# A two-layer mLSTM and retention trunk: head 0 reordered, its gate chain in pieces, and a first stage in another order

## The chip, the cores and the metric

The kernel runs on one core of one Trainium2 chip. The core has a matmul engine (PE, with its weight loads shown apart as PEld), a vector engine (DVE), an activation engine (ACT), a general engine (POOL) and a queue engine (SP) that here issues every transfer. The metric is the device time of one execution in microseconds. Each engine has its own stream of instructions and runs it in order; a semaphore holds an instruction back until its inputs are there.

## The reference

Two layers; each conditions a normalisation on a vector c, projects to gates, queries, keys and values, runs eight heads and projects back with a residual. Four heads are mLSTM, four are retention.

```python
for l in range(DEPTH):
    ada = silu(c) @ w_ada[l] + b_ada[l]
    shift, scale, gate = jnp.split(ada, 3, axis=-1)
    h = rmsnorm(x, norm_g[l]) * (1 + scale) + shift
    mq, mk, mv, mo, mz, mi, mf, rq, rk, rv, rz = split_cols(h @ w_in[l])
    qk = silu(causal_dwconv(concat([mq, mk]), conv_w[l], conv_b[l]))
    cell = mlstm_chunkwise(q, k, mv, mi + b_igate[l], mf + b_fgate[l])
    y_m = sigmoid(mo) * head_layernorm(cell, gn_m[l]) * silu(mz)
    ret = retention_chunkwise(rotary(rq), rotary(rk), rv)
    y_r = head_layernorm(ret, gn_r[l]) * silu(rz)
    x = x + gate * (concat([y_m, y_r]) @ w_out[l])
return rmsnorm(x, final_g)
```

Sequence 1024, model width 1024, head width 256, all float32. The mLSTM gates need, per head, running sums of log-sigmoids and a running maximum over the sequence; the kernel works in chunks of 256 tokens.

## The kernel before

Every product of float32 matrices is three matmuls of split operands (`mm3`, L134 to L136): each operand is cast to a high part (`split_to`, L574, mostly on ACT) and a low part, the rest of the subtraction (L575, mostly on POOL). A weight panel is a raw tile of 128 rows by 512 columns with its `wH` and `wL`. The hidden state `hT` lies transposed, eight slices of 128 model columns (k) by two halves of 512 tokens.

*The first stage* (L992 to L1067, layer 0) makes `hT` while the adaptive shift and scale come in. `ada_load` brings w_ada in four groups of 256 columns, `ada_group` (L216 to L226) accumulates each with multiply-adds by the activated c on DVE, `ada_sums` (L231) adds over partitions with matmuls, and `finish_gsh` (L201 to L204) turns the sums into `gsh`, shift and scale by column. The rows of x are squared with an accumulator on ACT (`squares`, L984), their root is taken over DVE and POOL (`row_rstd`, L923 to L926), the rows are scaled (`norm_scale`, L282 on ACT, L284 on DVE) and transposed by PE (L289), and each slice is split (`norm_split`: L295 or L297 with shift and scale, the high part L299 on ACT, the low part L300 on POOL). A step `first(half, k)` then multiplies one slice of one half by the z and o weights of head 0's first 128 columns, six matmuls of 512 columns. x comes in two halves, `xts[0]` and `xts[1]`. All of this stage's instructions are written out in order for all engines; behind it only PE's order is written out, and the other engines' orders come from the scheduler by the readiness that it computes.

*Units and launches.* Behind the first stage PE's stream is made of units: a projection of 128 columns (`proj_units`) is four units of 12 matmuls of 512 columns. `run_units` runs them one by one; each unit is a tick of a clock. `launch(generator, delay)` lets another generator take one step at each tick, from `delay` ticks on, up to its next `yield`; a `yield n` pauses it for n ticks. So the side work of a head (the gate chain, the value splits, the attention) is laid between the projections of the same or the next head.

*Head 0 of a layer*, in PE's order: z and o of the first 128 columns; z of the second 128 (`wz1`, L1077); the value units together with the gate columns (`v0_units` with `load_v0`, L1079); the gate chain launched (L1080); o of the second 128 (L1081); the query path and the key path with their convolutions (`conv_silu`: ACT L587, four DVE multiply-adds L592 and L594, ACT L596, DVE L597; keys split at L574, L575 and stored to DRAM); the value splits (`v0_splits`, L560 to L564, scaled by the gates) launched between the query and the key path with a delay of 2 (L1097); the attention launched with a delay of 2 (L1105); and head 1's paths go on beside it.

`gate_chain` (L417) runs on four partitions by 512: activations with Ln and Exp on ACT (L426 to L434), then for two halves some fifteen DVE operations each (L441 to L460, two sums and a maximum as scans among them), `yield 12`, and then transposes by PE (L468) and the small tables made from them. `attention` (L695) has, for four chunks j, `scores(j)` (matmuls of keys by queries, DVE products with the decay `dm`, L727 to L730, and a split into `sH` and `sL`), `values(j)` (matmuls of `sH`, `sL` by the values, and from the second chunk by the state) and `update(j)` (the state). In the attention it says

```python
scores(0)
yield 1
scores(1)
yield 1
for j in range(NCH):
    values(j)
```

Of the kernel before, what the change touches and what calls it, by code (L numbers as in the profile page):

```python
# [11 lines left out]
F32 = mybir.dt.float32  # L12
# [57 lines left out]
def tile_hybrid_trunk(ctx, tc, x, c, positions, w_ada, b_ada, norm_g, w_in, conv_w, conv_b,  # L70
# [92 lines left out]
    def load_cols_raw(l):  # L163
        rows = wt("rows", P, 2)
        Q.dma_start(rows[0:8, :], norm_g[l].rearrange("(r c) -> r c", c=P))
        Q.dma_start(rows[8:24, :], conv_b[l].rearrange("(r c) -> r c", c=P))
        Q.dma_start(rows[24:88, :], conv_w[l].rearrange("t (r c) -> (t r) c", c=P))
        Q.dma_start(rows[88:96, :], gn_m[l].rearrange("(r c) -> r c", c=P))
        Q.dma_start(rows[96:104, :], gn_r[l].rearrange("(r c) -> r c", c=P))
        Q.dma_start(rows[104:128, :], b_ada[l].rearrange("(r c) -> r c", c=P))  # L170
# [5 lines left out]
    def load_cols(l, rb):  # L176
        rows, bg = rb
        pt = ps_a()
        PE.transpose(pt[:, 0:P], rows, ident)
        cl = cst.tile([P, P], F32, tag=f"cols{l}", name=f"cols{l}")  # L180
        V.tensor_copy(cl, pt[:, 0:P])
        V.tensor_scalar(cl[:, 88:96], cl[:, 88:96], 0.25, None, ALU.mult)
        V.tensor_scalar(cl[:, 96:104], cl[:, 96:104], 0.5, None, ALU.mult)
        cols[l] = (cl, bg)
# [31 lines left out]
    def ada_group(raws, acc, parts):  # L216
        for part in parts:
            for a in range(2):
                kk = part * 2 + a
                for which in range(2):  # L220
                    aw = acc[:, which * 256:(which + 1) * 256]
                    rr = raws[part * 2 + which][:, a, :]
                    if kk == 0:
                        V.tensor_scalar(aw, rr, cact[:, 0:1], None, ALU.mult)
                    else:
                        V.scalar_tensor_tensor(aw, rr, cact[:, kk:kk + 1], aw, ALU.mult, ALU.add)  # L226
# [65 lines left out]
    def norm_split(l, pt, hT, half, k, on_act=False):  # L292
# [7 lines left out]
        G.tensor_tensor(hL, hf, f(hH), ALU.subtract)  # L300
# [80 lines left out]
    def load_v0(l):  # L381
# [3 lines left out]
        w = []  # L385
        for k in range(KT):
            raw = wt("raw", 512, 4)[:, 0:HD]
            Q.dma_start(raw, w_in[l, k * P:(k + 1) * P, OFF_MV:OFF_MV + HD])
            wH, wL = bt(F32R, HD + 8), bt(F32R, HD + 8)
            split_to((wH[:, HD:], wL[:, HD:]), gr[:, k * 8:(k + 1) * 8])  # L390
            split_to((wH[:, 0:HD], wL[:, 0:HD]), raw)
            w.append((wH, wL))
        return w
# [23 lines left out]
    def gate_chain(l, pgs, gt):  # L417
# [4 lines left out]
        fbs, lis_, es = [], [], []  # L422
        for half in range(2):
# [6 lines left out]
            fbs.append(fb)  # L430
# [4 lines left out]
        on4 = bt()  # L435
        V.memset(on4[0:4], 1.0)
        T4s = []
        for half in range(2):
            fb, li, e = fbs[half], lis_[half], es[half]
            lf, lfq = fb, bt()  # L440
            V.scalar_tensor_tensor(lf[0:4], fb[0:4], 0.0, e[0:4], ALU.min, ALU.subtract)  # L441
# [5 lines left out]
            liq, lir = bt(), bt()  # L447
# [3 lines left out]
            T4, uh, mx = bt(), bt(), bt()  # L451
# [5 lines left out]
            Q.dma_start(mdr[l][:, half * HALF:(half + 1) * HALF], mx[0:4])  # L457
            V.tensor_copy(T4[64:68], mx[0:4])
            V.tensor_tensor(uh[0:4], bq[0:4], mx[0:4], ALU.add)
            V.tensor_tensor(T4[96:100], uh[0:4], br[0:4], ALU.add)  # L460
            prev = {"bq": bq[0:4, 511:512], "br": br[0:4, 511:512], "mx": mx[0:4, 511:512]}
            T4s.append(T4)
        yield 12
# [231 lines left out]
    def attention(l, hg, gt, qT, kT, kt, vs, gp, rot):  # L695
# [138 lines left out]
        yield 1  # L834
# [146 lines left out]
    def squares(xt, ss, tts):  # L981
        for tt in tts:
            for cc in range(2):
                A.activation(wt("th", 512, 5), xt[tt][cc], AF.Square, accum_out=ss[:, tt, cc:cc + 1])  # L984
# [11 lines left out]
    crb = load_cols_raw(0)  # L996
    araw = [ada_load(0, 0)]
    rz, ro = [w_raw(zcol(0, 0), 0)], [w_raw(ocol(0, 0), 0)]
    xts.append(load_x(1))
    araw.append(ada_load(0, 1))  # L1000
    rz.append(w_raw(zcol(0, 0), 1))
    ro.append(w_raw(ocol(0, 0), 1))
    araw.append(ada_load(0, 2))
    araw.append(ada_load(0, 3))
    rz1 = [w_raw(zcol(0, 1), p) for p in range(2)]

    load_cact(crow)
    squares(xts[0], xss[0], range(4))
    accs = [bt()]
    norm_scale(xts[0], row_rstd(xss[0], "nrm"), range(4))  # L1010
    ada_group(araw[0], accs[0], (0,))
    load_cols(0, crb)
    ada_group(araw[0], accs[0], (1, 2, 3))
    wz, wo = split_w(rz[0], P), split_w(ro[0], P)

    for l in range(DEPTH):
        gt = {}
        gp = [[None, None], [None, None]]
        if l > 0:
# [10 lines left out]
        if l == 0:  # L1030
            pad = ps_a()
            seq = [(half, k) for g in range(4) for half in range(2) for k in (2 * g, 2 * g + 1)]
            for i in range(len(seq) + 2):
                if i == 2:
                    first(*seq[0])
                if i < len(seq):
                    half, k = seq[i]
                    pt = norm_transpose(xts[half], k)
                if i == 0:
                    ada_sums(0, 0, accs[0], pad)  # L1040
                if i > 2:
                    first(*seq[i - 2])
                if i in (4, 7, 11):
                    ada_sums(0, (i + 1) // 4, accs[-1], pad)
                if i < 2:
                    squares(xts[1], xss[1], ((0,), (1, 2))[i])
                if i < len(seq):
                    norm_split(0, pt, hT, half, k, i >= 2)
                if i == 1:
                    squares(xts[1], xss[1], (3,))  # L1050
                    accs.append(bt())
                    ada_group(araw[1], accs[1], range(1))
                    norm_scale(xts[1], row_rstd(xss[1], "nrm"), (2, 3))
                    ada_group(araw[1], accs[1], range(1, 4))
                if i in (4, 7):
                    accs.append(bt())
# [111 lines left out]
```

## Time and profile before

| | |
|---|---|
| Median of 3 runs | 2414.77 us (2414.24 to 2415.23) |
| Profiled execution | 2414.32 us, its span 2412.3 us |
| Mean granted clock of PE | 0.984 |
| Busy: PE, DVE, ACT, POOL | 2323.1, 1261.5, 896.2, 916.4 us |

The span runs from the first to the last instruction; some 2 us of the execution lie around it. Busy shares are means over stages that have different limits, so what a change of one stage is worth has to be read in that stage: in the table of stretches, and in PE's order of time, where brackets name the idle time ahead of an instruction and the work that ended it. PE runs at a granted clock; where it is below 1, the same matmul takes longer.

### The profile page before, as it was taken

To read this page: it belongs to the slowest core of one execution; us is meant where nothing else is said; L and a number is where in the kernel's file an instruction comes from. 1 tells how busy PE (TensorE), PEld (TensorE's weight loads), DVE (VectorE), ACT (ScalarE), POOL (GpSimd) and SP (SyncE) were. 2 spreads that over 40 slices of the span, in tenths; PEclk is the share of its full clock that TensorE was granted. 3 is DMA by queue.
4 is the path that set the end of the run, shared out by engine and by line. 5 is a ranking of instruction groups with operands and counts; after the bars stand their busy time and mean duration, and the time that the engine had idled before them with its cause. 6 is when DMAs were issued, how large, how long until landed. Compare 5 with 4: busy or idle time off the path is not lost.

```text
span 2412.3 us, 34405 instructions
## 1 busy us (share of the span) xinstructions
PE 2323.1 (96%) x12595; PEld 1993.0 (83%) x12595; DVE 1261.5 (52%) x2643; ACT 896.2 (37%) x1744; POOL 916.4 (38%) x861
## 2 busy tenths in 40 slices
PE   5997999999999999999999899999999999999998
PEld 3876888988988988978878678888898888888886
DVE  6184774555553444475624745454543445455763
ACT  5543354433322322243434434444442322224442
POOL 4443343333344343323452433443333443341313
PEclk9998999999999999999999999999999999999999
DMA  7223233433333333267522232323232323424772
GB/s 247 62 57 81 66 97 74 112 85 102 115 105 79 110 83 106 78 214 256 182 79 64 64 82 70 77 81 75 68 93 66 92 75 97 113 79 155 260 236 79
DMA packets 326105, 260.49 MB, mean 108 GB/s; under 512 B 75796, under 2 KB 260380, under 8 KB 325936
## 3 DMA queue, kind: packets, MB, share of 16 engines
q1 hardware_dynamic: 325936, 258.30, 36.9%
q8 instruction: 99, 1.62, 0.3%
q14 instruction: 70, 0.57, 0.1%
HBM read 202.61 MB, written 55.61 MB: 107 GB/s over the span
## 4 chain that ended last, share of the span: by engine, by line
PE 86%; DVE 6%; DMA 3%; ACT 2%; issue 2%; POOL 1%; SPq 1%; POOLq 0%; ACTq 0%; DVEq 0%
PE pp L135 22%; PE pp L134 22%; PE pp L136 22%; PE pa L136 6%; PE pa L134 6%; PE pa L135 6%; PE pa L725 1%; DMA b<-in_w_ada_dram 1%; DVE acc L592 1%; POOL b L300 0%; DVE b L561 0%; DMA b<-in_x_dram 0%; DVE acc L597 0%; DMA dm<-mdr 0%; DMA g<-gdr 0%
## 5 line engine op out<-in xcount | busy, mean ns | idle before, releaser
L134 PE MATMUL pp<-b,wH 128*128 128x512 f32 x1792 | 714.3, 399 | 8.3 <-DVE acc L592 5.3
L135 PE MATMUL pp<-b,wH 128*128 128x512 f32 x1792 | 712.4, 398 | 4.0 <-POOL b L300 4.0
L136 PE MATMUL pp<-b,wL 128*128 128x512 f32 x1792 | 712.1, 397 | 0.0
L575 POOL TENSOR_TENSOR wL<-raw,wH 128x512 fp32r<-128x512 f32 x338 | 458.6, 1365 | 601.5 <-ACT wH L574 487.5
L134 PEld LDWEIGHTS pp<-b,wH 128*128 128x128 f32 x1792 | 341.2, 190 | 83.7 <-issue 7.7
L136 PEld LDWEIGHTS pp<-b,wL 128*128 128x128 f32 x1792 | 339.8, 190 | 79.9
L135 PEld LDWEIGHTS pp<-b,wH 128*128 128x128 f32 x1792 | 340.4, 190 | 78.1 <-POOL b L300 5.9
L574 ACT CAST wH<-raw 128x512 fp32r<-128x512 f32 x402 | 246.6, 617 | 406.9 <-PE pp L135 156.8
L134 PE MATMUL pp<-wH,b 128*128 128x256 f32 (+1 forms) x1152 | 354.8, 308 | 3.7 <-ACT b L868 3.7
L136 PE MATMUL pp<-wH,b 128*128 128x256 f32 (+1 forms) x1152 | 354.3, 308 | 3.4 <-DVE b L869 3.4
L135 PE MATMUL pp<-wL,b 128*128 128x256 f32 (+1 forms) x1152 | 353.7, 307 | 0.0
L575 POOL TENSOR_TENSOR b<-acc,b 128x256 fp32r<-128x256 f32 (+1 forms) x192 | 177.2, 943 | 289.5 <-ACT b L574 278.2
L136 PEld LDWEIGHTS pp<-wH,b 128*128 128x128 f32 x1152 | 217.9, 189 | 15.8 <-DVE b L869 4.3
L134 PEld LDWEIGHTS pp<-wH,b 128*128 128x128 f32 x1152 | 218.4, 190 | 14.9 <-ACT b L868 4.1
L135 PEld LDWEIGHTS pp<-wL,b 128*128 128x128 f32 x1152 | 218.4, 190 | 11.0
L592 DVE SCALAR_TENSOR_TENSOR acc<-pp,cols,acc 128x511 f32<-128x511 f32 (+2 forms) x192 | 142.0, 742 | 52.7 <-ACT acc L587 50.9
L574 ACT CAST b<-acc 128x256 fp32r<-128x256 f32 (+1 forms) x192 | 83.6, 476 | 186.2 <-DVE acc L669 137.9
L575 POOL TENSOR_TENSOR sL<-th,sH 128x384 fp32r<-128x384 f32 x64 | 67.1, 1049 | 152.5 <-ACT sH L574 117.7
L134 PE MATMUL pa<-b,b 128*128 128x256 f32 (+1 forms) x320 | 91.7, 286 | 13.9 <-ACT b L574 10.6
L134 PE MATMUL pa<-wH,b 128*128 128x512 f32 x256 | 101.0, 395 | 0.0
L136 PE MATMUL pa<-wH,b 128*128 128x512 f32 x256 | 100.9, 394 | 0.0
L135 PE MATMUL pa<-wL,b 128*128 128x512 f32 x256 | 100.8, 394 | 0.0
(230 smaller groups left out, 3457.7 us busy)
## 6 DMA issues: line engine op xcount, KB each, us to landing
raw<-in_w_in_dram SPq DMA_DIRECT2D x274, 256.0 KB
raw<-in_w_out_dram SPq DMA_DIRECT2D x128, 256.0 KB
b<-in_w_ada_dram SPq DMA_DIRECT2D x96, 256.0 KB
gdr<-g SPq DMA_DIRECT2D x64, 256.0 KB
ndr<-zt SPq DMA_DIRECT2D x128, 128.0 KB
g<-ndr SPq DMA_DIRECT2D x64, 256.0 KB
g<-gdr SPq DMA_DIRECT2D x64, 256.0 KB
acc<-kdr SPq DMA_DIRECT2D x192, 64.0 KB
```

What stands on the lines that cost most here:

```text
L134: PE.matmul(o, lt[0], rt[0], start=start, stop=False)
L135: PE.matmul(o, lt[0], rt[1], start=False, stop=False)
L136: PE.matmul(o, lt[1], rt[0], start=False, stop=stop)
L574: A.copy(dst[0], src)
L575: eng.tensor_tensor(dst[1], src, f(dst[0]), ALU.subtract)
L592: V.scalar_tensor_tensor(acc[:, d:], pt[:, 0:HALF - d], wcol, acc[:, d:], ALU.mult, ALU.add)
L725: PE.matmul(pd, kk[i][:, jo + P:jo + CH], qd, start=dt == 0 and i == 0, stop=dt == 1 and i == 1)
```

## The change

1. *Small loads.* The eight small transfers of a layer's columns become two early ones (norm weight and adaptive bias, `load_ada_rows`, `ada_cols`) and six late ones (`load_head_rows`, `head_cols`).
2. *Adaptive weights.* Each group is still eight transfers of 256 KB, but each holds 128 rows of shift and scale columns together, so a multiply-add covers 512 columns in place of two of 256.
3. *Order of the transfers* in the first stage: the z and o panels go between the groups, x1 behind group 1, the gate columns and the first four value panels behind group 3, the second z panels after the stage.
4. *Order of the stage.* A written script of steps (T transpose, S split, F first, A multiply-adds, D sums, W and V weight splits, N squares and scaling of x1) takes the place of the loop. The steps with groups 0 and 1 go first for half 0, then for half 1; groups 2 and 3 alternate. The low part of `norm_split` is on DVE in place of POOL here. Squares of x0 are shared between ACT and DVE, all those of x1 are on ACT. Value weights are split in the last steps.
5. *Order of head 0 in both layers:* the value units come right behind the first z and o, the gate chain is launched with a delay of 1, then z and o of the second 128 columns.
6. *The gate chain* yields between its DVE operations in six places per half, and uses its buffers again.
7. *Attention of head 0:* the value splits are launched behind the key path with a delay of 1, the attention with a delay of 4 in place of 2, and a pause of 2 in place of 1 follows `scores(1)`. The rotary tables go from head 0 with a delay of 22 to head 1 with a delay of 18.

```diff
     def ada_load(l, g):
         raws = []
-        for part in range(4):
-            for which in range(2):
-                raw = bt().rearrange("p (a b) -> p a b", a=2)
-                Q.dma_start(raw, w_ada[l, part * 256:(part + 1) * 256, which * D + g * 256:which * D + (g + 1) * 256]
-                            .rearrange("(a p) b -> p a b", p=P))
-                raws.append(raw)
+        for kk in range(KT):
+            raw = bt()
+            Q.dma_start(raw.rearrange("p (w c) -> p w c", w=2),
+                        w_ada[l, kk * P:(kk + 1) * P].rearrange("p (w c) -> p w c", c=D)[:, 0:2, g * 256:(g + 1) * 256])
+            raws.append(raw)
         return raws
...
+    def ada_group(raws, acc, kks):
+        for kk in kks:
+            if kk == 0:
+                V.tensor_scalar(acc, raws[0], cact[:, 0:1], None, ALU.mult)
+            else:
+                V.scalar_tensor_tensor(acc, raws[kk], cact[:, kk:kk + 1], acc, ALU.mult, ALU.add)
...
-    def norm_split(l, pt, hT, half, k, on_act=False):
+    def norm_split(l, pt, hT, half, k, on_act=False, eng=G):
...
-        G.tensor_tensor(hL, hf, f(hH), ALU.subtract)
+        eng.tensor_tensor(hL, hf, f(hH), ALU.subtract)
...
         for half in range(2):
             A.activation(es[half][0:4], es[half][0:4], AF.Ln, bias=ones[0:4, 0:1])
+        yield 1
...
+            yield 1
             V.tensor_tensor_scan(bq[0:4], on4[0:4], lfq[0:4], prev.get("bq", 0.0), ALU.mult, ALU.add)
             V.tensor_tensor_scan(br[0:4], on4[0:4], lf[0:4], prev.get("br", 0.0), ALU.mult, ALU.add)
+            yield 1
...
-        yield 12
+            yield 1
+        yield 3
...
         scores(0)
         yield 1
         scores(1)
-        yield 1
+        yield 2 if hg == 0 else 1
...
+    def squares(xt, ss, on_dve):
+        for tt in range(4):
             for cc in range(2):
...
+                if tt in on_dve:
+                    V.scalar_tensor_tensor(o, xt[tt][cc], 1.0, xt[tt][cc], ALU.mult, ALU.mult,
+                                           accum_out=ss[:, tt, cc:cc + 1])
...
+            script = ("T0 D0 W0 T1 S0 S1 A10-8 T2 F0 F1 D1 S2 T3 S3 N F2 F3 A20-6 T4 S4 A26-8 T5 S5 D2 W1 T6 S6 F4 T7 S7 F5 "
+                      "T8 S8 F6 A30-3 T9 S9 F7 A33-6 T10 S10 F8 A36-8 T11 S11 F9 D3 V0 T12 S12 F10 V1 T13 S13 F11 V2 "
+                      "T14 S14 F12 V3 T15 S15 F13 V4 F14 V5 F15 V6 V7")
...
+        vraw = []
+        run_units(v0_units(l, load_v0(l) if l else w0, hT, vraw, pgs))
+        launch(gate_chain(l, pgs, gt), 1)
...
         run_units(proj_units(wz1, hT, z_evac(gp, 1)))
-        vraw = []
-        run_units(v0_units(l, load_v0(l), hT, vraw, pgs))
-        launch(gate_chain(l, pgs, gt))
...
-                if hg == 0 and which:
-                    launch(v0_splits(gt, vraw, vs), 2)
...
-            launch(attention(l, hg, gt, qT, kT, kt, vs, gp, rot), 2 if hg == 0 else 0)
+            if hg == 0:
+                launch(v0_splits(gt, vraw, vs), 1)
+            launch(attention(l, hg, gt, qT, kT, kt, vs, gp, rot), 4 if hg == 0 else 0)
...
-            if hg == 0 and l == 0:
-                launch(rotary_tables(), 22)
+            if hg == 1 and l == 0:
+                launch(rotary_tables(), 18)
```

More of the change, by code (lines that the diff above doesn't have):

```diff
@@ L384, in load_v0, with v0_raw, v0_split @@
                     w_in[l, :, OFF_I:OFF_I + 8].rearrange("(k p) g -> p k g", p=P))
[L385 to L393, printed above, removed]
+        return gr
+    def v0_raw(l, k):
+        raw = wt("raw", 512, 4)[:, 0:HD]
+        Q.dma_start(raw, w_in[l, k * P:(k + 1) * P, OFF_MV:OFF_MV + HD])
+        return raw
+    def v0_split(gr, raw, k):
+        wH, wL = bt(F32R, HD + 8), bt(F32R, HD + 8)
+        split_to((wH[:, HD:], wL[:, HD:]), gr[:, k * 8:(k + 1) * 8])
+        split_to((wH[:, 0:HD], wL[:, 0:HD]), raw)
+        return wH, wL
+    def load_v0(l):
+        gr = v0_gates(l)
+        return [v0_split(gr, v0_raw(l, k), k) for k in range(KT)]
     def v0_units(l, w, hT, vraw, pgs):
@@ L1030, in tile_hybrid_trunk @@
         if l == 0:
[L1031 to L1056, printed above, removed]
-                    ada_group(araw[len(accs) - 1], accs[-1], range(4))
-                if i == 3:
-                    wz += split_w(rz[1], P)
-                    wo += split_w(ro[1], P)
@@ new lines, in tile_hybrid_trunk @@
+            for step in script.split():
+                n = int(step[1] if step[0] == "A" else step[1:] or 0)
+                if step[0] == "T":
+                    pts[n] = norm_transpose(xts[seq[n][0]], seq[n][1])
+                elif step[0] == "S":
+                    norm_split(0, pts.pop(n), hT, *seq[n], on_act=n >= 2, eng=V)
+                elif step[0] == "F":
+                    first(*seq[n])
+                elif step[0] == "A":
+                    if len(accs) == n:
+                        accs.append(bt())
+                    ada_group(araw[n], accs[n], range(int(step[2]), int(step[4])))
+                elif step[0] == "D":
+                    ada_done(n)
+                elif step[0] == "N":
+                    squares(xts[1], xss[1], ())
+                    norm_scale(xts[1], row_rstd(xss[1], "nrm"), (0, 2))
+                elif step[0] == "V":
+                    w0.append(v0_split(vgr, vrw[n], n))
+                    if n + 4 < KT:
+                        vrw.append(v0_raw(0, n + 4))
+                else:
+                    wz += split_w(rz[n], P)
+                    wo += split_w(ro[n], P)
@@ L1062, in tile_hybrid_trunk @@
+            rz1 = [w_raw(zcol(0, 1), p) for p in range(2)]
+            head_cols(0, hrows)
             startup.__exit__(None, None, None)
-            wz1 += split_w(rz1[1], P)
-            load_cols(1, load_cols_raw(1))
         else:
```

112 lines of the change are left out of this document (63 added, 49 removed).

## The prediction

> **What bounds the kernel now.** I read the page's head first, then the waits of the matmul engine (PE), then a table of stretches, then the order of time inside the stretches that lose.
>
> ```profile
> span 2412.3 us, 34405 instructions
> ...
> PE 2323.1 (96%) x12595; PEld 1993.0 (83%) x12595; DVE 1261.5 (52%) x2643; ACT 896.2 (37%) x1744; POOL 916.4 (38%) x861
> ```
>
> PE is busy for 96% of the span, so there are 89 us of holes to win (2412.3 less 2323.1), and besides them the matmuls that run at a lowered clock. The whole-run waits of PE say who makes the holes; columns are the waiting line, the releaser, microseconds in all, times, the longest.
>
> ```profile
> PE pa L134 <- ACT sH L574: 12.1, 2, 6.0
> PE pa L134 <- ACT b L574: 10.6, 2, 5.3
> ...
> PE pp L134 <- DVE acc L592: 5.3, 2, 2.8
> PE pa L136 <- POOL sL L575: 4.3, 2, 2.2
> ...
> PE pa L136 <- POOL b L575: 1.1, 2, 0.6
> ```
>
> Five of these rows come twice, and the two times are alike: once in each layer, at head 0. They sum to 33.4 us (12.1 + 10.6 + 5.3 + 4.3 + 1.1). Most of the rows left out belong to the first stage. Now the stretches (us, then busy time of PE, weight load, DVE, ACT, POOL, granted clock, DMA share, GB/s):
>
> ```profile
> 0.00:76.90 76.90, 46.65 (x196) 35.36 (x196) 40.62 (x98) 45.20 (x87) 36.74 (x32) 0.93 0.61 194
> 112.70:146.00 33.30, 33.30 (x144) 26.68 (x143) 27.45 (x36) 16.09 (x22) 10.14 (x9) 1.00 0.18 44
> 211.00:270.00 59.00, 59.00 (x314) 50.57 (x313) 27.17 (x72) 22.81 (x46) 21.27 (x22) 1.00 0.28 75
> 270.00:300.00 30.00, 30.00 (x131) 24.27 (x130) 25.33 (x43) 11.37 (x21) 11.24 (x11) 1.00 0.22 62
> 1300.00:1400.00 100.00, 83.36 (x352) 67.11 (x350) 71.69 (x142) 46.56 (x88) 36.80 (x36) 0.90 0.25 61
> ```
>
> The first stage fills PE for 46.65 of 76.9 us; from 112.7 to 146 and from 211 on PE is full. Between 146 and 211 come three holes, each followed by matmuls at a lower clock; the row of 1300 to 1400 is head 0 of layer 1, at a mean clock of 0.90. The holes in PE's order of time (start, duration, and in brackets the idle time and who ended it):
>
> ```profile
> 145.45 0.39 PE L135 MATMUL pp<-b,wH 128*128 128x512 f32 x1
> 145.69 0.40 PE L136 MATMUL pp<-b,wL 128*128 128x512 f32 x1
> 148.84 0.62 PE L134 MATMUL pp<-b,wH 128*128 128x512 f32 x1 [2.76 <-DVE acc L592]
> 149.25 0.63 PE L135 MATMUL pp<-b,wH 128*128 128x512 f32 x1
> ...
> 152.57 0.40 PE L134 MATMUL pp<-b,wH 128*128 128x512 f32 x1
> ...
> 179.29 0.28 PE L135 MATMUL pa<-b,b 128*128 128x256 f32 x1
> 179.41 0.28 PE L136 MATMUL pa<-b,b 128*128 128x256 f32 x1
> 185.02 0.58 PE L134 MATMUL pa<-b,b 128*128 128x256 f32 x1 [5.33 <-ACT b L574]
> ...
> 190.08 0.39 PE L134 MATMUL pp<-b,wH 128*128 128x512 f32 x1
> ...
> 195.20 0.40 PE L136 MATMUL pp<-b,wL 128*128 128x512 f32 x1
> 201.64 0.58 PE L134 MATMUL pa<-b,sH 128*128 128x258 f32 x1 [6.04 <-ACT sH L574]
> ...
> 210.48 0.39 PE L135 MATMUL pp<-b,wH 128*128 128x512 f32 x1
> ```
>
> A full-clock matmul of 512 columns starts 0.235 us behind the one before (145.45 to 145.69; 0.232 over longer rows of them), one of 256 columns 0.12 us (179.29 to 179.41); behind the first hole they start 0.41 to 0.43 us apart (148.84, 149.25). What a hole costs is then the time between two full-clock starts less the nominal time of the matmuls between them.
> - 145.69 to 152.57: 6.88 us, ten matmuls of 512 (2.32): lost 4.56.
> - 179.41 to 190.08: 10.67 us, eight of 256 (0.96) and six of 512 (1.39): lost 8.32.
> - 195.20 to 210.48: 15.28 us, eleven of 512 (2.55) and nine of 258 (1.08): lost 11.65.
>
> Layer 0's head 0 thus loses 24.5 us, of which the five waits are 16.8 (2.76, 5.33, 6.04, and from the last two rows of the waits 2.1 and 0.6). Layer 1's are 33.4 - 16.8 = 16.6; at the same ratio 24.2 us.
>
> The Trainium skill, "TensorE: Matmul & The Clock Gate", Part 1, says that an idle window of about 3.4 us drops the array to half clock and that as long a busy time brings it back. The rows agree on the half clock, but the 2.76 us wait already dropped it. By that rule alone the restart would cost 1.7 us a hole, and a layer 16.8 + 5.1 = 21.9 us.
>
> **The change, part by part.** Now who is late in each hole.
>
> ```profile
> 118.84 0.68 DVE L441 SCALAR_TENSOR_TENSOR b<-b,b 4x512 f32<-4x512 f32 x1 [5.20 <-ACT b L434]
> ...
> 145.08 0.68 DVE L460 TENSOR_TENSOR b<-b,b 4x512 f32<-4x512 f32 x1
> ...
> 145.85 2.06 DVE L592 SCALAR_TENSOR_TENSOR acc<-pp,cols,acc 128x511 f32<-128x511 f32 x3
> ...
> 166.72 0.69 DVE L597 SCALAR_TENSOR_TENSOR acc<-th,acc 128x512 f32<-128x512 f32 x1 [0.76 <-ACT th L596]
> ...
> 178.30 1.92 DVE L561 SCALAR_TENSOR_TENSOR b<-b,eul,b 128x256 fp32r<-128x256 f32 x2
> 180.14 1.22 DVE L564 CAST b<-eH 128x4 fp32r<-128x4 f32 x1
> ...
> 198.37 0.39 DVE L727 TENSOR_TENSOR th<-pa,dm 128x256 f32<-128x256 f32 x1
> ```
>
> *Gate chain in pieces, value units ahead of z1.* DVE runs the chain in one block from 118.84 to 145.76, and the first convolution stands behind it at 145.85. Afterwards the chain starts behind the value units with both z1 and o1 still to come, each four units of 12 matmuls (2.78 us), and the query path behind these. Call the end of the value units V. Logarithms on ACT take to V+7.3 (here 111.5 to 118.84), the 27 us chain with evacuations between its pieces to about V+30 to V+38; the first query half leaves PE at V+28.9, and the chain's transposes are due at V+41.8. The wait goes, with some 2 to 4 us to spare for the transposes. The same instructions and table loads are issued, some buffers fewer: nothing else to pay. Gain 4.6 in layer 0.
>
> *Value splits behind the key path.* The splits of L561 and L564 stand between the key convolutions on DVE (the last at 178.30 and 180.14, 1.92 and 1.22 long); they hold up the key half whose cast on ACT scores(0) await until 185.02. Moved behind the key path, and the scores two units later (5.6 us, more than the 5.33 of wait), this wait goes: 8.3. Their own user is values(0).
>
> *Values one unit later.* sH was late because scores(0), once late, gave DVE their products only from 198.37 on. Counting from the key path's end K, sH is then cast at K+20.6, sL is ready at K+21.7 and values(0) start at K+21.9. That is 0.2 us of slack, so I keep a residue: 0 to 4 us a layer (6.0 + 2.1 was the wait, half of it is the upper end), taken as 2.
>
> *Rotary tables* go from head 0 to behind head 1: same work beside full PE, with DVE busy 25.33 of 30 us there (270 to 300). Between 0 and +2; taken 0, as PE lost nothing in that row. Layer 1's small loads go behind the value units, eight transfers and two transposes, no one waits soon: 0.
>
> *First stage.* Its rows, by group (count | busy, mean ns), and PE's pace:
>
> ```profile
> L226 DVE SCALAR_TENSOR_TENSOR b<-b,cact,b 128x256 f32<-128x256 f32 x56 | 27.9, 569 | 0.9 <-DMA b<-in_w_ada_dram 0.9
> L300 POOL TENSOR_TENSOR b<-acc,b 128x512 fp32r<-128x512 f32 x16 | 27.0, 1698 | 20.3 <-ACT b L299 20.2
> L984 ACT ACTIVATE th<-b 128x512 f32<-128x512 f32 x16 | 10.0, 625 | 2.5 <-DMA b<-in_x_dram 2.4
> L224 DVE TENSOR_SCALAR b<-b,cact 128x256 f32<-128x256 f32 x8 | 2.6, 349 | 4.5 <-DMA b<-in_w_ada_dram 4.5
> ...
> 13.00:46.00 33.00, 18.17 (x69) 12.54 (x69) 22.68 (x55) 21.16 (x43) 14.79 (x10) 1.00 1.09 354
> ...
> 69.88 0.60 PE L289 MATMUL pa<-ident,b 128*128 128x128 f32 x4
> 71.70 0.60 PE L289 MATMUL pa<-ident,b 128*128 128x128 f32 x4
> ...
> 43.27 0.78 ACT L295 ACTIVATE acc<-pa,gsh 128x512 f32<-128x512 f32 x1 [5.04 <-DVE gsh L204]
> ...
> 40.66 2.50 POOL L575 TENSOR_TENSOR wL<-b,wH 128x512 fp32r<-128x512 f32 x2
> ```
>
> 64 multiply-adds of 256 (30.5 us) become 32 of 512; at the 0.69 of L597 (166.72), of that width, 22. The 16 low-part subtractions leave POOL (27.0) for DVE: 16 x 0.69 = 11. DVE also takes four of 16 squares (4 x 0.69 = 2.8). DVE rises by 5.3 (22 + 11 + 2.8 - 30.5) from 40.62 in 76.9: it still fits. The bytes stay; at 354 GB/s a 256 KB piece takes 0.74 us. Six small transfers leave the head of the queue, so group 0's sums end about 2.5 us sooner. But the written order puts x1's eight squares on ACT behind the splits S2, S3, which wait for group 1's shift and scale. My walk: group 0 accumulated 18.5, shift and scale 21, S0 and S1 to 25.2, group 1 (8 x 0.62, starts overlapping) 30.2, its sums 32.2, S2 and S3 on ACT (each 0.78 and a cast) 34.9, eight squares (0.625 and a readout each) 40.3, their root over POOL 41.9, x1 scaled 44, group 2 (behind it on DVE, with S4, S5) 49.1, F4 at 51.4. From there PE has twelve steps F4 to F15 at 1.82 us (69.88 to 71.70), 21.8, and about 2 of restart: the stage ends at 75.2 against 76.9. Gain 1.7. Bounds: last transfers land at 46, plus group 3's tail, 2.3 of sums and six steps gives 58 to 60 (gain 17); if all 11 us of subtractions lie on the path, against 5 that their absence from POOL saves, it loses 5. I take the walk. The value weights' early splits only have to be ready by the end of the stage; they are the last written in it: 0 to +2, in the range.
>
> The Trainium skill, "SBUF — State Buffer" (the single rule on contention), says that a DVE operation with two SBUF inputs and a POOL operation lock each other out. It speaks against the subtractions on DVE: by it the 12 weight splits left on POOL (1.25 us each, 40.66) could block DVE for at most 15 us, and the stage would end at 90. The rows lean to it as a partial effect: L226 averages 569 ns, L224, with one SBUF tensor less, 349; no row tells how much of that lies on the path.
>
> Sum: 2414.32 (the profiled run; 2.0 us lie around its span, and the median 2414.77 is 0.45 above it) - 24.5 - 24.2 - 1.7 + 2 x 2 = 2367.9. The two residues are the only debits.
>
> **The rivals.**
> 1. *The wait for sH stays or returns.* For: 0.2 us of slack, and the splits of the values now stand on DVE and ACT beside it. Against: scores three units earlier relative to values. If the third hole stays in both layers (11.65 x 2, less the residues of 4): 2367.9 + 19.3 = 2387.
> 2. *The first stage follows its transfers.* For: POOL's 27.0 us are off the path, DMA at 354 GB/s until 46 and the pieces land in the order of use. Against: x1's squares behind S3. Gain 10 to 17 there, say 12 instead of 1.7: 2357.6.
> 3. *Slower.* Group 0's attention steps come later and run beside head 1's query and key convolutions, where DVE has 25.33 of 30 us full (270 to 300 is such a stretch). If each of its eleven steps a layer (four scores, four values, three updates) waited 2.1, as sL now makes PE wait, plus a restart of 1.7: 22 x 3.8 = 84, so 2367.9 + 84 = 2452. It decides from 13 steps on (13 x 3.8 = 49 against 46 to lose). Against: most of these steps run in 211 to 270 before, and PE has no hole there.
> 4. *It doesn't do what it says*: the chain's pieces are moved but the scheduler leaves DVE's order, so that the first two holes stay (12.9 x 2): 2393.7.
>
> **How the numbers follow.** Forecast 0.48, rival 1 0.17, rival 2 0.15, rival 3 0.09, rival 4 0.07, and mixtures within 0.2% (4.8 us, about what a measurement can tell) 0.04. Predicted is the first: 2368. Its own range is 2362 to 2376. For 8 in 10 the range goes from rival 2's lower bound (2367.9 - 15 = 2353) to rival 4 with a small margin, 2397. Faster: 0.48 + 0.17 + 0.15 + 0.07 = 0.87; same 0.04; slower 0.09.
>
> **What would show it.** Right: PE's waits for acc L592, b L574, sH and sL gone or under 1 us each, the clock 1.00 from 77 to 210 and in layer 1's head 0, the last step of the first stage near 75 with ACT's squares from 35 to 40. Wrong: a wait of PE for sH or sL over 2 us; a stage end near 60 or beyond 80; DVE multiply-adds of 512 at over 0.9 us; new waits in 210 to 300.

## The result and the profile after

The changed kernel takes 2383.95 us (median of four runs, 2382.69 to 2384.54); the kernel before, beside it, 2414.51 us. The ratio is 0.9874, with a 95% interval of 0.9857 to 0.9891. It is faster by 30.6 us, where 46.4 were forecast. The profiled run took 2383.42 us, its span 2381.7 us.

The page's head, and PE's waits over the whole run (line, releaser, microseconds in all, times, longest):

```profile
span 2381.7 us, 34373 instructions
...
PE 2314.3 (97%) x12597; PEld 1988.5 (83%) x12597; DVE 1270.6 (53%) x2643; ACT 893.3 (38%) x1734; POOL 889.1 (37%) x845
...
PE pa L238 <- DVE b L233: 17.4, 4, 6.5
...
PE pa L296 <- ACT b L289: 6.9, 4, 3.3
PE pp L134 <- DVE b L581: 6.9, 1, 6.9
...
PE pa L134 <- ACT sH L594: 2.6, 1, 2.6
...
PE pa L136 <- POOL sL L595: 1.9, 3, 0.7
```

The five waits of head 0 are gone but for some 0.6 us each for sL. Two waits have grown: for the adaptive multiply-adds (L233, in the first stage) from 5.6 to 17.4 us, and a new one of 6.9 us for a value split (L581); the wait of 2.6 us for sH is new too and lies in head 1's stretch, between 300 and 500. The stretches that answer to those of before (us, busy time of PE, weight load, DVE, ACT and POOL, granted clock, DMA share, GB/s):

```profile
0.00:83.50 83.50, 47.04 (x194) 36.76 (x195) 48.33 (x93) 41.24 (x87) 17.20 (x25) 0.84 0.55 178
107.00:150.00 43.00, 43.00 (x193) 34.72 (x192) 34.79 (x53) 20.69 (x30) 14.98 (x13) 1.00 0.22 57
150.00:212.00 62.00, 61.38 (x294) 50.80 (x293) 41.45 (x105) 33.55 (x73) 27.00 (x28) 1.00 0.32 80
430.00:450.00 20.00, 13.13 (x82) 11.85 (x82) 17.11 (x28) 8.42 (x16) 6.63 (x5) 0.83 0.31 79
450.00:500.00 50.00, 46.85 (x251) 40.11 (x250) 37.59 (x91) 23.32 (x45) 18.51 (x22) 0.97 0.41 116
1300.00:1400.00 100.00, 99.32 (x478) 82.43 (x477) 69.42 (x154) 45.56 (x96) 47.56 (x47) 1.00 0.34 85
```

PE is full from 107 to 150 and all but full to 212, and in layer 1 as well (99.32 of 100 at clock 1.00, against 83.36 at 0.90). The first stage ends at 83.5 in place of 76.9. And from 430 to 500 there are 10 us of idle PE where head 1 runs.

Counted as in the prediction (time between starts less the nominal time of the matmuls between), layer 0 lost 24.8 us from 76.9 to 300 before and 1.8 us from 83.5 to 300 now: 23.0 won. In the first stage 6.7 us more are lost. From 300 to 500, where the rotary tables are made, 5.9 us were lost before and 13.7 now: 7.8 more. Layer 1 wins the rest: the first cast of the output projection (the line at L868 before, L888 after) starts 9.2 us sooner in layer 0 (1025.9 to 1016.7) and the span is 30.6 us shorter, so 21.4 are left for all that lies behind it, above all layer 1. So the heads gave 44.4 of the 44.7 us forecast; the missing 16 us lie in the first stage and at the tables.

### The profile page after: what moved, and what is told of

It reads as the page before. It is cut to its first block, busy times and chain, and to the rows that moved or that the text cites. A ratio compares the mean times of both kernels' runs of the same rounds, so it can differ in the third digit from the quotient of the medians.

```text
span 2381.7 us, 34373 instructions
## 1 busy us (share of the span) xinstructions
PE 2314.3 (97%) x12597; PEld 1988.5 (83%) x12597; DVE 1270.6 (53%) x2643; ACT 893.3 (38%) x1734; POOL 889.1 (37%) x845
## 4 chain that ended last, share of the span: by engine, by line
PE 90%; DVE 4%; DMA 3%; issue 1%; ACT 1%; SPq 0%; POOL 0%; POOLq 0%; DVEq 0%; ACTq 0%
PE pp L134 23%; PE pp L135 23%; PE pp L136 23%; PE pa L136 6%; PE pa L134 6%; PE pa L135 6%; PE pa L745 1%; DMA b<-in_w_ada_dram 1%; DVE acc L612 1%; DMA b<-in_x_dram 0%; PE pa L296 0%; DVE b L233 0%; DVE acc L617 0%; DMA g<-gdr 0%; DMA b<-in_w_in_dram 0%
## 5 line engine op out<-in xcount | busy, mean ns | idle before, releaser
L595 POOL TENSOR_TENSOR wL<-raw,wH 128x512 fp32r<-128x512 f32 x338 | 451.7, 1343 | 607.6 <-ACT wH L594 472.2
L616 ACT ACTIVATE th<-acc 128x512 f32<-128x512 f32 x64 | 40.5, 632 | 136.8 <-DVE acc L614 79.6
```

Source lines behind the costliest of these rows:

```text
L595: eng.tensor_tensor(dst[1], src, f(dst[0]), ALU.subtract)
L616: A.activation(th, acc, AF.Tanh, scale=0.5)
```

## The experiments

Medians are set against the changed kernel's 2383.95 us; single runs of one kernel spread by 1 to 8 us. Ratios are to the kernel before, which ran beside each (medians 2412.5 to 2414.2), so a difference of 2 us or less says nothing by itself.

**The rotary tables back at head 0** (`rotary_back`).

```diff
-            if hg == 1 and l == 0:
-                launch(rotary_tables(), 18)
+            if hg == 0 and l == 0:
+                launch(rotary_tables(), 22)
```

> The changed kernel, with the rotary tables launched at head 0 with a delay of 22 again. Theory: at head 1 the tables stand between the value splits of head 1 on DVE and make a new hole of PE (6.9 us and a cold restart, 12.6 us lost from 430 to 500 where the kernel before lost 1.3), and at head 0 they cost 4.6 us; so this kernel gains 7 to 8 us on the changed one, 2376. Rival: the hole at 436 to 443 comes from the later attention of head 0, not from the tables; then the hole stays and the time is 2380 to 2389.

Measured 2375.37 us (ratio to before 0.9835, interval 0.982 to 0.985): 8.6 us faster than the changed kernel. The hole at 436 is gone; in its place are two waits of 1.7 us each for L791 (3.4 in all), as the kernel before had. PE, DVE and POOL of the changed kernel, in order of time, show how the hole came about:

```profile
436.30 0.28 PE L136 MATMUL pp<-wH,b 128*128 128x256 f32 x1
443.45 0.79 PE L134 MATMUL pp<-b,wH 128*128 128x512 f32 x1 [6.87 <-DVE b L581]
444.04 0.63 PE L135 MATMUL pp<-b,wH 128*128 128x512 f32 x1
```

```profile
434.13 1.75 DVE L360 TENSOR_TENSOR b<-b,b 128x512 f32<-128x512 f32 x1
435.80 2.32 DVE L646 SCALAR_TENSOR_TENSOR b<-acc,wd,b 128x256 fp32r<-128x256 f32 x3
438.05 1.48 DVE L362 TENSOR_SCALAR b<-b 128x512 f32<-128x512 f32 x1
439.45 1.48 DVE L646 SCALAR_TENSOR_TENSOR b<-acc,wd,b 128x256 fp32r<-128x256 f32 x1
440.85 0.68 DVE L363 SCALAR_TENSOR_TENSOR b<-b,b 128x512 f32<-128x512 f32 x1
441.45 0.47 DVE L581 SCALAR_TENSOR_TENSOR b<-pp,eul,b 128x256 fp32r<-128x256 f32 x1
441.85 0.68 DVE L364 SCALAR_TENSOR_TENSOR b<-b,b 128x512 f32<-128x512 f32 x1
...
442.58 0.41 DVE L367 TENSOR_SCALAR b<-b 128x512 f32<-128x512 f32 x1
442.92 0.47 DVE L581 SCALAR_TENSOR_TENSOR b<-pp,eul,b 128x256 fp32r<-128x256 f32 x1
```

```profile
436.57 4.07 POOL L595 TENSOR_TENSOR wL<-raw,wH 128x512 fp32r<-128x512 f32 x3 [1.24 <-ACT wH L594]
```

Each value unit's sums lie in a `pp` tile until L581 has read them. DVE reached L581 only at 441.45, behind three operations of the tables (L360, L362, L363) and the key rows (L646), and the split that ended PE's wait at 442.92, behind two more (L364, L367). PE ran out of free tiles at 436.3. Some of these operations were stretched while POOL computed low parts: L362 took 1.48 us where L367, of the same kind and width, took 0.41; L360 took 1.75 where L370, also a subtraction of 512 columns, took 0.69 at 444.65. With two of the key rows these stretches make some 4 us of the delay (an estimate from the like rows), so the tables' own work isn't all of it.

**The tables moved, in the kernel before** (`rotary_moved_alone`): the same edit the other way round, in the kernel before.

```diff
-            if hg == 0 and l == 0:
-                launch(rotary_tables(), 22)
+            if hg == 1 and l == 0:
+                launch(rotary_tables(), 18)
```

> The kernel before, with the rotary tables at head 1 with a delay of 18. Theory: the new hole comes from the tables' place alone, 7 to 8 us slower than before: 2422. Rival: it needs the attention of head 0 laid later, then within 3 us of before.

Measured 2423.3 us against 2414.18 (1.0035, 1.0023 to 1.0048): 9.1 slower. PE's waits from 212 to 500:

```profile
PE pp L134 <- DVE b L561: 6.6, 1, 6.6
PE pa L134 <- ACT sH L574: 2.6, 1, 2.6
PE pa L136 <- POOL sL L575: 0.3, 1, 0.3
```

It is the same hole, with the heads as they were: the tables' place makes it, not the later attention.

**The old first stage** (`old_stage`): the first stage, its transfers and its order are those of before; the value weights are loaded and split at its end. The lines are set against the kernel before.

```diff
+    vgr = v0_gates(0)
+    vrw = [v0_raw(0, k) for k in range(4)]
...
             seq = [(half, k) for g in range(4) for half in range(2) for k in (2 * g, 2 * g + 1)]
             for i in range(len(seq) + 2):
...
+                if i >= 12 and len(w0) < 4:
+                    n = len(w0)
+                    w0.append(v0_split(vgr, vrw[n], n))
+                    vrw.append(v0_raw(0, n + 4))
```

> The changed kernel with the first stage of the kernel before (transfers of small rows ahead, multiply-adds of 256 columns, order in turn by half, low part on POOL); only the value weights are loaded and split at its end in place of the second z weights. Theory: the new first stage ends 6.7 us later than the old one (83.5 against 76.9), so this gains about 6.7 us: 2377. Rival: the value splits at the end of the stage, not the order, make it longer; then this one is no faster than the changed kernel (2382 to 2386).

Measured 2376.1 us (0.9844, 0.983 to 0.986): 7.9 faster than the changed kernel. The value units start at 78.23; they start at 83.56 in the changed kernel, while the stage of the kernel before ended at 76.9. So by the traces 5.3 of the 6.7 us belong to the new stage itself; the other 1.3 come with the value splits at the end, where PE waits 0.9 us for a low part on POOL (L300) in the last step. The medians say 7.9, within the spread of this kernel's runs (2374.2 to 2380.7).

**Head 0 alone** (`heads_only`): both edits together, that is, parts 5, 6 and 7 of the change without its first stage and without the tables' move.

> Both of the two kernels beside it at once: the reordered heads 0 alone, with the first stage and the rotary tables of before. Theory: head 0's 23.0 us in layer 0 and 22 in layer 1 are all that the change gains, so 2414.5 - 45 = 2369.5. Rival: the first stage and the tables interact with the holes, and part of the 45 comes back: over 2375.

Measured 2367.92 us (2367.73 to 2369.01; 0.9809, 0.9794 to 0.9823). The two edits add up: 7.9 and 8.6 make 16.5, and 16.0 were measured. This kernel is faster than both, and than the changed kernel: of the whole change, parts 5 to 7 without the tables' move were worth having, the rest cost 16 us.

**The squares of x1 sooner** (`squares_early`).

```diff
-"... A10-8 T2 F0 F1 D1 S2 T3 S3 N F2 F3 ..."
+"... A10-8 T2 F0 F1 D1 Q S2 T3 S3 N F2 F3 ..."
+                elif step[0] == "Q":
+                    squares(xts[1], xss[1], ())
                 elif step[0] == "N":
-                    squares(xts[1], xss[1], ())
```

> The changed kernel; only the eight squares of the second half of x stand ahead of the splits S2 and S3 on ACT in place of behind them. Theory: x1 landed at about 30 but its squares ran from 38.0 to 43.1 because S2 and S3 waited for group 1's shift and scale; now they run while ACT waits, the root comes some 4 to 5 us sooner, and so do group 2 and the twelve steps behind it: 2379. Rival: group 2's multiply-adds and their low-part subtractions on DVE pace the stage, not the scaled x1; then under 1 us: 2383 to 2384.

Measured 2379.79 us (2377.94 to 2381.59), 4.2 less; by the trace the value units start at 80.49, 3.1 us sooner. The place of the squares costs 3 to 4 us of the stage.

**The low parts on POOL** (`low_on_pool`).

```diff
-                    norm_split(0, pts.pop(n), hT, *seq[n], on_act=n >= 2, eng=V)
+                    norm_split(0, pts.pop(n), hT, *seq[n], on_act=n >= 2, eng=G)
```

> The changed kernel; only the first stage's 16 low-part subtractions go back from DVE to POOL. Theory that DVE paces: groups 2 and 3 no longer have subtractions between their multiply-adds, the wait for group 3's sums (2.6 us) goes and group 2 ends 1 to 2 us sooner: 2380 to 2381. Rival that the lock between the two engines and POOL's 1.3 us a subtraction cost more: 2385 to 2390.

Measured 2379.83 us (2378.3 to 2381.42), 4.1 less; by the trace the value units start at 82.25, 1.3 us sooner, and the runs' spread covers the difference between the two. It doesn't get slower, then; a gain of 1 to 4 us is all that can be said. DVE and PE of this kernel:

```profile
45.03 9.02 DVE L233 SCALAR_TENSOR_TENSOR b<-b,cact,b 128x512 f32<-128x512 f32 x7
...
54.11 1.87 PE L238 MATMUL pa<-ones,b 128*128 128x1 f32 x8 [7.64 <-DVE b L233]
```

PE's wait for group 3's sums is gone, as the theory said. But group 2's seven multiply-adds, now beside POOL's subtractions, took 9.02 us, against 7.3 in the changed kernel, and PE waited 7.64 us for them. Group 2 ended only 0.4 us sooner, where the theory had 1 to 2: what DVE was spared came back as stretching.

**The attention of head 0 early again** (`attention_early`).

```diff
+                if hg == 0 and which:
+                    launch(v0_splits(gt, vraw, vs), 2)
...
-        yield 2 if hg == 0 else 1
+        yield 1
...
-            if hg == 0:
-                launch(v0_splits(gt, vraw, vs), 1)
-            launch(attention(l, hg, gt, qT, kT, kt, vs, gp, rot), 4 if hg == 0 else 0)
+            launch(attention(l, hg, gt, qT, kT, kt, vs, gp, rot), 2 if hg == 0 else 0)
```

> The changed kernel with head 0's value splits between the query and the key path again, its attention with a delay of 2 and no added pause; the order of the value units and the divided gate chain stay. Theory: the second and third hole (8.3 and 11.65 us in layer 0, the like in layer 1) come back for the most part: plus 30 to 40, 2414 to 2424. Rival: they were late because the gate chain blocked DVE, and with the chain out of the way less than half comes back: 2386 to 2404.

Measured 2422.02 us: 38.1 slower than the changed kernel and slower than before (1.0038, 1.0023 to 1.0053). PE's waits from 83 to 300:

```profile
PE pa L134 <- ACT sH L594: 6.0, 1, 6.0
PE pa L134 <- ACT b L594: 5.8, 1, 5.8
PE pa L136 <- POOL sL L595: 2.2, 1, 2.2
PE pa L136 <- POOL b L595: 0.6, 1, 0.6
```

The second and third hole are back at their old size, though the gate chain is out of the way and the first hole stays away. These two holes come from the place of the attention and the value splits, not from the chain.

**Only the value splits early** (`splits_early`): of the last diff the four lines on `v0_splits` alone; the delays and the pause stay.

> The changed kernel with only head 0's value splits between the query and the key path again; its attention stays late. Theory: what took the second and third hole away is the later start of the scores and values, in front of which even delayed key convolutions are ready; the splits' place costs little: within 3 us, 2381 to 2387. Rival: the splits hold up the last key half by more than the two units: a hole for scores(0) comes back in both layers, 2 to 6 us each, 2388 to 2396.

Measured 2389.21 us (2386.62 to 2391.48), 5.3 slower. In each layer there are waits of 0.2 to 0.4 us for the key cast, 0.8 for its low part and 1.3 for sL. The time lies in the rival's range, not in the theory's, though the waits for scores(0), 1.0 to 1.2 us a layer, are shorter than the rival's 2 to 6. So with the scores late the splits' place costs some 5 us, and with the splits early the late scores and values are worth the other 33 of the 38.1. What the moved splits are worth with the scores early was not run.

**The gate chain in one piece** (`chain_in_one`): none of its yields (five in each half, and one ahead of the halves), a pause of 14 behind its operations.

> The changed kernel with the gate chain undivided (all operations at one tick, then 14 ticks of pause), behind the early value units. Theory: the early place is what takes the first hole away, the pieces do little: within 3 us, 2381 to 2387. Rival: an undivided 27 us on DVE holds up the evacuations of the second z and o columns, which then stop PE in both layers: 2390 to 2400.

Measured 2385.46 us (2383.39 to 2386.67): 1.5 slower, less than the runs spread. The chain's operations ran from 116.25 to 143.8 and the first convolution at 146.36, without a wait of PE over 1.3 us in either layer's head 0. The division does nothing that can be measured here.

**The value units behind the second z columns again** (`values_after_z1`).

```diff
-        vraw = []
-        run_units(v0_units(l, load_v0(l) if l else w0, hT, vraw, pgs))
-        launch(gate_chain(l, pgs, gt), 1)
...
         run_units(proj_units(wz1, hT, z_evac(gp, 1)))
+        vraw = []
+        run_units(v0_units(l, load_v0(l) if l else w0, hT, vraw, pgs))
+        launch(gate_chain(l, pgs, gt), 1)
```

> The changed kernel with the second z columns ahead of the value units again, the gate chain divided and launched behind the value units, head 0's attention late. Theory: the early value units remove the first hole; with them late the chain starts four units (11.1 us) later and its DVE work again meets the first convolutions and PE's transposes: 4 to 6 us lost in each layer, 2392 to 2396. Rival: dividing the chain is enough, as the convolutions can go between its pieces: 2383 to 2386.

Measured 2409.11 us (2405.71 to 2413.59): 25.2 slower, more than either theory said. PE's waits from 83 to 300:

```profile
PE pa L488 <- DVE b L478: 7.3, 1, 7.3
PE pa L193 <- DMA rows<-in_gn_r_dram: 6.4, 1, 6.4
PE pa L136 <- POOL sL L595: 0.6, 1, 0.6
```

The first is in both layers (14.5 us over the run): PE's transposes stand at their written place and the chain isn't ready, as on DVE the convolutions now run between its pieces (from 152.5 to 163.7 in layer 0). The second is this kernel's own: layer 1's small transfers now stand right behind the stage. Without its 6.4 us and some 2 of slow restart (an estimate from the first hole, 4.56 lost for 2.76 of wait) some 17 us stay, so with the chain in pieces the early place of the value units is worth more than the first hole's 4.6 us a layer.

**The first stage in another order** (`stage_rewritten`), with the tables at head 0.

```diff
+    xts.append(load_x(1))
     araw.append(ada_load(0, 1))
-    xts.append(load_x(1))
...
+            script = ("T0 D0 W0 T1 Q S0 S1 F0 F1 N A10-8 T2 S2 T3 S3 T4 F2 F3 D1 S4 A20-6 T5 S5 W1 T6 F4 S6 A26-8 T7 F5 S7 D2 "
+                      "T8 F6 S8 T9 F7 S9 A30-3 T10 F8 S10 A33-6 T11 F9 S11 A36-8 T12 F10 D3 S12 V0 T13 F11 S13 V1 T14 F12 S14 V2 T15 F13 S15 V3 V4 F14 V5 "
+                      "F15 V6 V7")
...
+                    norm_split(0, pts.pop(n), hT, *seq[n], on_act=True, eng=G if 2 <= n < 10 else V)
...
+                elif step[0] == "Q":
+                    squares(xts[1], xss[1], (1, 3))
+                    rs1 = row_rstd(xss[1], "nrm")
```

> The changed kernel with the rotary tables back at head 0 and another first stage: x1 ahead of group 1 in the transfers, steps in turn by half for each group, squares of x1 shared by ACT and DVE and put ahead of the first splits, all shift-and-scale steps on ACT, low parts of steps 2 to 9 on POOL and the others on DVE, each group's multiply-adds two steps ahead of their use. Theory: the stage is held by the order of work on DVE and ACT, not by its transfers (last piece at 46) nor by PE; with F0 at 26 and twelve steps of 1.83 us behind group 1 at 37 it ends at 60 to 65, 18 to 23 us ahead of the changed kernel's 83.5; with the tables' 8 us: 2352 to 2358. Rival: the locking of POOL and DVE stretches each step to over 2.5 us whatever the order: the stage ends at 72 to 80 and the time is 2366 to 2373.

Measured 2368.46 us (2366.7 to 2371.12). The value units start at 76.70: 6.9 us sooner than in the changed kernel, but by no means at 60; the rival's numbers came out. DVE and POOL of this kernel, in order of time:

```profile
30.21 6.39 DVE L233 SCALAR_TENSOR_TENSOR b<-b,cact,b 128x512 f32<-128x512 f32 x7
40.92 9.96 DVE L233 SCALAR_TENSOR_TENSOR b<-b,cact,b 128x512 f32<-128x512 f32 x7
```

```profile
42.09 3.19 POOL L307 TENSOR_TENSOR b<-acc,b 128x512 fp32r<-128x512 f32 x2 [4.33 <-ACT b L306]
45.24 3.42 POOL L595 TENSOR_TENSOR wL<-b,wH 128x512 fp32r<-128x512 f32 x2
48.63 3.41 POOL L307 TENSOR_TENSOR b<-acc,b 128x512 fp32r<-128x512 f32 x2
```

Group 2's seven multiply-adds took 9.96 us. The first two ran ahead of POOL and started 0.79 us apart; the other five ran beside it and took some 1.68 us each. POOL's pairs took 3.2 to 3.4 us, where a pair alone takes 2.5.

**The same with all low parts on DVE** (`stage_dve`), two multiply-adds between each, group 1's sums ahead of F2 and the value splits two steps sooner.

```diff
-                    norm_split(0, pts.pop(n), hT, *seq[n], on_act=True, eng=G if 2 <= n < 10 else V)
+                    norm_split(0, pts.pop(n), hT, *seq[n], on_act=True, eng=V)
```

> The rewritten first stage, again with the rotary tables at head 0, but with all 16 low parts on DVE, two multiply-adds between each, so that POOL has nothing to do beside DVE but the second z and o weights and the value weights; group 1's sums ahead of F2. Theory: in the stage before it seven multiply-adds beside POOL's subtractions took 9.96 us (1.42 each against 0.66 alone) and these subtractions 1.6 to 1.7 in place of 1.3; without them group 2 is ready at about 46 and group 3 at 54 to 57, and the stage ends at 63 to 67 in place of 76.7: 2355 to 2360. Rival: 16 subtractions in DVE's order cost as much as the lock did; the stage ends at 74 to 80, 2366 to 2372.

Measured 2366.82 us (2365.49 to 2372.78); the value units start at 76.04. The rival's numbers came out. PE waited for groups 2 and 3 as in the changed kernel (first DVE's subtraction of the sixth slice, S5, then PE):

```profile
41.76 0.69 DVE L307 TENSOR_TENSOR b<-acc,b 128x512 fp32r<-128x512 f32 x1 [2.50 <-ACT b L306]
...
50.00 1.86 PE L238 MATMUL pa<-ones,b 128*128 128x1 f32 x8 [5.64 <-DVE b L233]
64.74 1.05 PE L238 MATMUL pa<-ones,b 128*128 128x1 f32 x8 [1.55 <-DVE b L233]
```

DVE's subtraction at 41.76 waited 2.50 us for ACT, ACT had waited 2.95 us for PE's transpose (until 40.29), and PE's transpose stands behind the step before; the multiply-adds laid behind the subtraction on DVE waited along. Three orders of the stage (old, rewritten, all on DVE) end at 78.2, 76.7 and 76.0, and the three kernels take 2367.9, 2368.5 and 2366.8 us, which their runs don't tell apart. What would bring the stage near its transfers' end at 46 wasn't found.

## Why the prediction was right and wrong

The measured 2384 us lies above the forecast's own range (2362 to 2376) and inside the wide one (2353 to 2397). No rival describes what happened there: it is the forecast with two terms wrong, some 8 us each and both to the slow side. That the time still falls inside the wide range is luck, since its bounds were drawn from rivals that didn't happen. Of the signs named beforehand, the waits of head 0 went as hoped, while a stage end beyond 80 and multiply-adds over 0.9 us (beside POOL) showed the first stage wrong, and the wait of 2.6 us for sH the tables.

*Right: head 0.* Forecast were 24.5 and 24.2 us less a residue of 2 in each layer, 44.7 in all; the traces give 23.0 and 21.4, and `heads_only` is 46.3 us faster than the kernel before beside it. The method that gave them, the time between two full-clock starts less the nominal time, held to within a few us. The residue for sH was too dear: 0.6 us of waiting for sL a layer was left. Without the two residues the forecast would have been 48.7, so that 44.7 fits this closely is in part luck.

*Right in size, partly wrong in cause: what makes each hole.* "Value splits behind the key path" put the second hole down to the splits that stand between the key convolutions on DVE. With the splits early and the attention late (`splits_early`) the hole's own two waits are only 1.2 us (0.4 and 0.8) in layer 0, so the two units more take it away without the moved splits; whether the moved splits alone would do isn't shown. "Gate chain in pieces, value units ahead of z1" was half right: the early value units do it, the pieces don't (1.5 us). And the cost of having them late was underrated: with the chain in pieces it is the transposes, not the convolution, that wait (7.3 us).

*Wrong: "First stage ... my walk".* It gave a gain of 1.7 us (end at 75.2); the stage lost 6.7 (end at 83.5), beyond the walk's worse bound of 5. The steps were the right ones, each came late, and two terms were mis-sized. DVE, POOL, ACT and PE of the changed kernel:

```profile
27.35 5.48 DVE L233 SCALAR_TENSOR_TENSOR b<-b,cact,b 128x512 f32<-128x512 f32 x7
51.08 3.42 DVE L233 SCALAR_TENSOR_TENSOR b<-b,cact,b 128x512 f32<-128x512 f32 x2
...
50.64 3.32 POOL L595 TENSOR_TENSOR wL<-b,wH 128x512 fp32r<-128x512 f32 x2 [6.12 <-ACT wH L594]
...
42.32 0.61 ACT L1009 ACTIVATE th<-b 128x512 f32<-128x512 f32 x1
...
54.56 1.86 PE L238 MATMUL pa<-ones,b 128*128 128x1 f32 x8 [6.46 <-DVE b L233]
72.49 1.05 PE L238 MATMUL pa<-ones,b 128*128 128x1 f32 x8 [2.58 <-DVE b L233]
```

The walk took 0.62 us a multiply-add ("8 x 0.62, starts overlapping"). Without POOL beside them they take 0.78 (5.48 for 7); over the 24 of groups 0 to 2, 3 to 4 us. Two of group 2 took 3.42 us beside POOL's split of the second z and o weights, 1.9 more than alone; the walk had no term for that. So group 1 was done at 32.8 (walk 30.2), x1's squares at 42.9 (40.3), F4 began at 57.0 (51.4). And "twelve steps at 1.82" left out that group 3's multiply-adds stand between the subtractions on DVE: PE waited 2.58 us for them in the middle of the twelve. 5.6 and 2.6 make 8.2 of the 8.3 us missed. The walk's other support, that DVE "still fits", was an argument from a share: DVE was busy for 48.33 of 83.5 us, and PE waited 17.4 us for it. How much of the late start the squares' place behind S2 and S3 accounts for, `squares_early` shows (3 to 4 us); the prediction had named that place and priced it in its walk.

*Wrong: "Rotary tables ... taken 0".* The row of 270 to 300 (DVE busy 25.33 of 30, PE full) was taken for proof that the work hides there. That row isn't of the new place: in the kernel before, the tables' operations on DVE run from 282 to 356, so the row holds the first of them at their old place, while in the changed kernel they run from 384 to 472. And busy time alone doesn't tell: at head 1 the tables meet the value splits, which PE needs within a few us because they free its tiles. It cost 7.8 us by the traces, 8.6 by `rotary_back`, 9.1 by `rotary_moved_alone`, against a bound of 2. The step failed by an argument from a mean share of another stretch, where DVE's queue at the new place had to be asked for who stands behind.

*The rivals.* Rival 1 (sH stays) didn't happen. Rival 2 (the stage follows its transfers) didn't either, and two kernels written for it ended no earlier than 76.0. Rival 3, the slower one, didn't happen as written: holes did come behind DVE's queue in head 1, but only one of 6.9 us and one of 2.6, and the tables' place makes both (`rotary_moved_alone` has them, `rotary_back` has not). Rival 4 didn't happen: the first two holes are gone.

*The lock rule of the Trainium skill* ("SBUF — State Buffer", the single rule on contention), weighed in the prediction, agrees with the rows in kind: multiply-adds of 0.78 us alone took some 1.7 beside POOL (3.42 for 2), and POOL's own operations grew with them. The exclusion isn't a full one in these rows: in `stage_rewritten` POOL did two operations from 45.24 to 48.63, 3.39 us, beside two multiply-adds, where 2.5 and 1.6 one after the other would make 4.1. And it doesn't forbid the subtractions on DVE: on either engine the time was within some 4 us of the other.

## What to carry to other kernels

A hole in a busy engine is worth its wait plus the slow restart, read as time between two full-clock starts less nominal time; that held to a few us, and the cure here was to put more units between a late result and its use. What is moved to a "hidden" place has to be checked in the queue that it joins: not how busy that engine is there, but who stands behind it and how soon that is wanted. A written order over several engines runs at the pace of its chain of hand-overs; before it is walked through, the pitch of its operations has to be read from a row in which they stand as they will stand, in the same chain and with the same engines at work beside them.

## What the runs showed of the hardware that was not expected

Multiply-adds of 512 columns into one accumulator start 0.79 us apart in the changed kernel (seven take 5.48 us, each 0.75), while squares of the same width, each into a tile of its own, start 0.61 apart on DVE (in the last kernel from 22.16 to 24.00, four of them). That each waits for the sum of the one before is the likely reason; it wasn't tested, and the multiply-adds also read a column of c where the squares have a constant. At the head of a stretch at the low clock, PE's first matmuls of 512 columns start 0.73 and 0.59 us apart, more than the 0.43 of those that follow, in the changed kernel's first stage:

```profile
24.14 0.80 PE L134 MATMUL pp<-b,wH 128*128 128x512 f32 x1 [0.20 <-ACT b L306]
24.87 0.80 PE L135 MATMUL pp<-b,wH 128*128 128x512 f32 x1
25.46 0.63 PE L136 MATMUL pp<-b,wL 128*128 128x512 f32 x1
25.89 0.63 PE L134 MATMUL pp<-b,wH 128*128 128x512 f32 x1
```

A start 0.59 us behind the first stands behind the hole at 443.45 too. No run tells why.
